# Moving four groups of DMA issues in a one-core hybrid attention/mLSTM layer

## The chip, the cores and the metric

The kernel runs on one core of a Trainium2 chip, as one launch. The metric is the device time of a launch in microseconds (us), lower is better. A time is the median of several runs; one further run is taken with the hardware profiler, and its trace is what the profile shows.

## The reference

One layer of a bidirectional hybrid encoder: 2048 tokens of width 1024. A conditioning vector gives shift, scale and gate; the normalised input goes through one wide projection, whose columns feed two head groups with SiLU gates; one output projection, the residual, and a last RMSNorm follow.

```python
def reference(x, c, w_ada, b_ada, norm_w, w_in, b_in, conv_w, conv_b, rpb, ml_norm_w, w_out, final_norm_w):
    shift, scale, gate = jnp.split(silu(c) @ w_ada + b_ada, 3, axis=-1)
    h = rmsnorm(x, norm_w) * (1 + scale) + shift
    (na_q, na_k, na_v, na_z, ml_q, ml_k, ml_v, ml_o, ml_z, i_f, f_f, i_b, f_b) = split(h @ w_in + b_in)
    # 8 heads of 64: each token attends to 8 x 16 neighbours on a 32 x 64 grid, with a bias table
    na_out = neighbourhood_attention(na_q, na_k, na_v, rpb) * silu(na_z)
    # 4 heads of 128, in both directions; a short centred convolution on q and k first
    mq, mk = split(silu(centred_short_conv(concat(ml_q, ml_k), conv_w, conv_b)))
    hm = (mlstm(mq, mk, ml_v, i_f, f_f) + flipped mlstm(mq, mk, ml_v, i_b, f_b)) * sigmoid(ml_o)
    ml_out = headwise_norm(hm) * ml_norm_w * silu(ml_z)
    y = concat(na_out, ml_out) @ w_out
    return rmsnorm(x + gate * y, final_norm_w)
```

`mlstm` is a chunked recurrence: a state matrix per head is carried from chunk to chunk with a decay, and each chunk adds a masked product of its own queries, keys and values.

## The kernel before

**Number format.** The wide products take three matmuls for one: activations and weights are each split into a high and a low part (`hhi`/`hlo`, `whi`/`wlo`), and high·high, high·low and low·high are added up in PSUM. A weight block is loaded raw by DMA, ScalarE (ACT) copies out the high part, VectorE (DVE) or GpSimd (POOL) subtracts to get the low one.

**Stages, in order of time.** (1) `start`: modulation, norm, transposes and the first two token blocks. (2) The token stage, `tok_blocks`: blocks 2 to 5, each four groups of four token tiles; a token tile is 24 matmuls into one of four `pp` buffers and a DVE addition into a stage tile. Blocks 2 and 3 are mLSTM values and output gates (`vo_group`), blocks 4 and 5 the attention values V (`nav_group`, line 607 the addition, line 611 the store to `d_vna`). The stage tile alternates between two buffers, so the additions of a group wait until the store of the group before the last has landed. After each token tile one step of `self.chain` runs: first `gate_chain`, then `decays`. (3) `conv_blocks`: mLSTM keys and queries with their convolution, and the tables of attention biases (line 679). (4) `phase1b`: the mLSTM passes. Pass 1 builds the states of a head, pass 2 goes through its 16 chunks from c = 15 down to 0 and combines. Beside them `pump` puts out matmuls of a second product, `nq_gen`. (5) `phase2`: attention, 64 units in slots, with the output projection pumped in.

**Decays.** For each of 16 (head, group) pairs `decays` has a 128 x 1024 tile: loaded from `d_mneg` by two DMAs on SyncE's queue, SP (line 833), masked by POOL (841), exponentiated by ACT (845), stored to `d_ck` on ACT's queue (847). Two tiles take turns; the load of pair n + 2 goes into the tile that pair n leaves, and so waits until its store has landed.

**The side product.** `nq_gen` goes through a list of turns, 31 of them; a turn is one weight block of 128 columns and one to four of the groups of 512 tokens, and each of the 64 items (turn, group) is 24 matmuls on line 1001: for k = 0 to 7 the three of `(whi, hhi)`, `(whi, hlo)`, `(wlo, hhi)`, numbered n = 0 to 2. The last seven turns have one group each, but for one of two. The raw weights of the turn after next are held in a single buffer (`rawq`, tag raw0): at k = 2, n = 0 of the first item of a turn `nq_split` (lines 974/975, or 977/978 for the query weights, which it also scales) makes the next turn's halves of `whi_a` and `wlo_a`, and right after it `nq_load` (966) loads the raw weights of the turn after, when the split has read the buffer. The last of these loads, here called the last raw load, is that of turn 30; it is issued in item 61 and split in item 62.

**Pass 2.** Each chunk loads a `ck` tile on SP (1198). `load_z` (1207), also on SP, loads a tile `zt` of z for four chunks into one of two buffers and waits there for an older `zt` to be stored to `d_mix`.

**What sets the order.** DMAs are issued by the queues of SP, ACT and POOL, each in one fixed order, and a DMA that must wait holds up all behind it on its queue. Only `start` and the slots of `phase2` stand under `manual_schedule`; there every engine's order is that of the source. Everywhere else a planner makes each engine's order when the program is built: it follows its own estimate of when an instruction's inputs and buffers are ready, and source order decides between those that are ready together. The manual part of `phase2` begins in the middle of item 59 of the side product: slots 0 to 3 each put out a unit's scores (`stage_s`), the loads for later slots, and then `pump(22)`, 22 matmuls of the side product; slot 4 puts out the rest.

In slots 0 to 2 SP's order after the scores is

```python
load_tab(follows[u], j)          # 1457: bias table of a later unit, two per slot
load_q(n // 2 + 2)               # 1394, 1397: queries, three DMAs, in slot 2
1: [load_w(4), load_w(5)],       # 1460: rows of the output projection, hlo<-d_wo
2: [load_w(6), load_w(7), nc.sync.dma_start(zs[1], self.d_mix[b0])],   # 1460, 1629
```

and then whatever the pumped items issue.

Of the kernel before, what the change touches and what calls it, by code (L numbers as in the profile page):

```python
# [54 lines left out]
def patch_ps(ap):  # L55
    return ap.rearrange("p (a r k) -> p r a k", a=4, k=16)
# [6 lines left out]
class Kernel:  # L63
# [536 lines left out]
    def nav_group(self, blk, slot, g):  # L600
        nc = self.nc
        c0 = (blk - 4) * 256
        st = self.stage_tile(f"stv_{blk}_{g}")
        for o in range(4):
            ps = self.pp.tile([P, GT], F32, tag="pp", name=f"pv_{blk}_{g}_{o}")
            self.tok_tile(ps[:, :256], self.wslot[slot], 4 * g + o)
            nc.vector.tensor_add(st[:, o, :256], ps[:, :256], self.brows[blk % 2])  # L607
            next(self.chain, None)
        self.flush()
        dst = self.d_vna[g * GT : (g + 1) * GT, c0 : c0 + 256].rearrange("(o p) c -> p o c", p=P)  # L610
        self.defer(lambda: nc.sync.dma_start(dst, st[:, :, :256]))

# [203 lines left out]
    def decays(self, pool, beside):  # L816

        nc = self.nc
        mask = pool.tile([P, 2, CH], F32, name="mask")
        nc.gpsimd.memset(mask, 0.0)  # L820
        nc.gpsimd.affine_select(out=mask[:, 0, :], in_=mask[:, 0, :], pattern=[[1, CH]], compare_op=ALU.is_ge, fill=-BIG, base=0, channel_multiplier=-1)
        nc.gpsimd.affine_select(out=mask[:, 1, :], in_=mask[:, 1, :], pattern=[[-1, CH]], compare_op=ALU.is_ge, fill=-BIG, base=0, channel_multiplier=1)
        groups = [(h, gi) for h in range(MH) for gi in range(NG)]
        tiles = {}

        def load(n):
            h, gi = groups[n]
            flat = pool.tile([P, D], F32, tag=("wgate", "gacc")[n % 2], bufs=1, name=f"dec_{h}_{gi}")
            t = flat.rearrange("p (d c t) -> p d c t", d=2, c=4)
            for d in range(2):  # L830
                r = d * 64 + h * NC + 4 * gi
                src = self.d_mneg[:, r : r + 4].rearrange("e r t -> e (r t)").unsqueeze(1).broadcast_to([16, 8, 512])
                nc.sync.dma_start(flat[:, d * 512 : (d + 1) * 512], src)
            tiles[n] = t

        load(0)
        load(1)
        yield
        for n, (h, gi) in enumerate(groups):
            t = tiles.pop(n)  # L840
            nc.gpsimd.tensor_tensor(t, t, mask.unsqueeze(2).broadcast_to([P, 2, 4, CH]), ALU.add)  # L841
            for d in range(2):
                for o in range(4):
                    c = 4 * gi + o
                    nc.scalar.activation(t[:, d, o, :], t[:, d, o, :], AF.Exp, bias=self.cols["g"][:, d, h, c : c + 1])  # L845
                dst = self.d_ck[h, 4 * gi : 4 * gi + 4, :, 641 + d * CH : 641 + (d + 1) * CH].rearrange("c p t -> p c t")
                nc.scalar.dma_start(dst, t[:, d])
            yield
            next(beside, None)
            yield  # L850
            if n + 2 < len(groups):
                load(n + 2)
            yield
        for _ in beside:
            pass

# [123 lines left out]
    def nq_gen(self):  # L980
        nc = self.nc
        whi, wlo = self.wslot[0]
        both, upper, lower = range(NG), (3, 2), (1, 0)
        turns = [(s, both) for s in (0, 1, 2, 3)] + [(s, upper) for s in (4, 5, 6, 7, 8, 9, 10, 11, 12, 14, 13, 15)]
        turns += [(s, lower) for s in (8, 9, 10, 11, 4, 5, 6, 7)]
        turns += [(15, (1,)), (13, (1,)), (14, (1,)), (12, (1, 0)), (14, (0,)), (13, (0,)), (15, (0,))]
        order = [(i, s, g) for i, (s, gs) in enumerate(turns) for g in gs]
        needs = [i for i, (s, gs) in enumerate(turns) if i == 1 or i > 1 and s != turns[i - 2][0]]
        raw = self.nq_load(needs[0], turns[needs[0]][0])
        late, parity = [], False  # L990
        for i, s, g in order:
            off = (i % 2) * P
            kind, ct = ("mz", "nz", "k", "q")[s // 4], s % 4
            patch = kind != "k"
            col = {"mz": 20, "nz": 8, "k": 4, "q": 0}[kind] + ct
            bias = self.bcol[:, col : col + 1]
            ps = self.pp.tile([P, GT], F32, tag="pp", name=f"pq_{s}_{g}")
            for k in range(KT):
                w1, w2 = whi[:, k, off : off + P], wlo[:, k, off : off + P]
                for n, (w, h) in enumerate(((w1, self.hhi), (w1, self.hlo), (w2, self.hhi))):  # L1000
                    nc.tensor.matmul(patch_ps(ps) if patch else ps, w, self.htok(h, g, k, patch), start=(k == 0 and n == 0), stop=(k == KT - 1 and n == 2))  # L1001
                    if k == 2 and n == 0:
                        while late:
                            (nc.gpsimd if self.attention else nc.scalar).dma_start(*late.pop(0))
                    if k == 2 and n == 0:
                        if needs and needs[0] == i + 1:
                            needs.pop(0)
                            self.nq_split(*raw)
                            if needs:
                                raw = self.nq_load(needs[0], turns[needs[0]][0])  # L1010
                    if k < KT - 1 or n < 2:
                        yield
            if kind == "k" and g in lower:

                for j in range(2):
                    rows, other = slice(j * HD, (j + 1) * HD), slice((1 - j) * HD, (2 - j) * HD)
                    cols = slice(j * T + g * GT, j * T + (g + 1) * GT)
                    hv = self.kk[ct][rows, cols]
                    nc.scalar.activation(hv, ps[rows], AF.Identity, bias=bias[rows])
                    nc.vector.scalar_tensor_tensor(self.kk[ct][other, cols], ps[rows], bias[rows], hv.bitcast(F32), ALU.add, ALU.subtract)  # L1020
                yield
                continue
            parity = not parity
            if parity:
                both = self.qst.tile([P, 1032], F32R, tag="st", name=f"qst_{s}_{g}")
            else:
                both = self.raw.tile([P, 1024], F32R, tag="raw1", name=f"qst_{s}_{g}")
            hv, lv = both[:, 0:512], both[:, 512:1024]
            if kind in ("mz", "nz"):
                hv = hv.bitcast(F32)  # L1030
                nc.scalar.activation(hv, ps, AF.Silu, bias=bias)
                dst = self.d_zna[4 * g : 4 * g + 4, :, ct].rearrange("a p q -> p a q") if kind == "nz" else self.d_zml[ct, g]
                nc.scalar.dma_start(dst, hv.rearrange("p (a q) -> p a q", a=4))
                self.zdone.add((kind, ct, g))
            else:
                nc.scalar.activation(hv, ps, AF.Identity, bias=bias)
                nc.vector.scalar_tensor_tensor(lv, ps, bias, hv.bitcast(F32), ALU.add, ALU.subtract)
                for e, part in enumerate((hv, lv)):
                    src = part.bitcast(F32).rearrange("p (a q) -> p a q", a=4)
                    if kind == "q":  # L1040
                        dst = self.d_qna[e, ct // 2, 4 * g : 4 * g + 4, :, ct % 2].rearrange("a p q -> p a q")
                    else:
                        dst = self.d_kna[e, ct * P : (ct + 1) * P, g * GT : (g + 1) * GT].rearrange("p (a q) -> p a q", a=4)
                    late.append((dst, src))
            if (s, g) in ((15, 3), (15, 2)):
                self.freed.append(g)
            yield
        while late:
            nc.gpsimd.dma_start(*late.pop(0))
# [141 lines left out]
    def ml_pass2(self, ml, h):  # L1191
# [11 lines left out]
        def load_z(gi):  # L1203
            while ("mz", h, gi) not in self.zdone:
                self.pump(1)
            t = ml.tile([P, 4, CH], F32, tag="zt", bufs=2, name=f"zt_{h}_{gi}")
            nc.sync.dma_start(t, self.d_zml[h, gi])
            zt[gi] = t
# [87 lines left out]
        last = NC - 1  # L1296
# [6 lines left out]
        for c in range(last, -1, -1):  # L1303
# [5 lines left out]
                scores(c - 1)  # L1309
                weigh(c - 1)  # L1310
            self.pump(PUMP2 / 2)
            if c % 4 == 0:
                load_z(c // 4)
            combine(c)
            if c < last:
                moments(c + 1)
# [469 lines left out]
```

## Time and profile before

| what | us |
|---|---|
| runs | 1330.75, 1332.98, 1333.43 |
| median | 1332.98 |
| the profiled run, as timed | 1336.63 |
| its span, first to last instruction | 1334.6 |
| outside the span | 2.0 |
| DVE busy in it | 781.6 |
| ACT busy in it | 592.9 |
| POOL busy in it | 236.1 |

The profiled run is 3.65 us above the median; differences are worked out inside it and then put on the median. A row of a timeline gives the start, the duration, the engine (a q behind it: its issuing queue), the line, and what is written and read; a bracket holds idle time before the instruction and what ended it. A row of waits gives the waiter, the releaser, the total, the count and the longest. A row of windows gives, for a stretch of time, the busy time of each engine with its instructions in brackets, then TensorE's granted clock, the busy share of the 16 DMA engines (it can pass 1, as packets overlap) and GB/s.

### The profile page before, as it was taken

To read this page: it belongs to the slowest core of one execution; us is meant where nothing else is said; L and a number is where in the kernel's file an instruction comes from. 1 tells how busy PE (TensorE), PEld (TensorE's weight loads), DVE (VectorE), ACT (ScalarE), POOL (GpSimd) and SP (SyncE) were. 2 spreads that over 40 slices of the span, in tenths; PEclk is the share of its full clock that TensorE was granted. 3 is DMA by queue.
4 is the path that set the end of the run, shared out by engine and by line. 5 is a ranking of instruction groups with operands and counts; after the bars stand their busy time and mean duration, and the time that the engine had idled before them with its cause. 6 is when DMAs were issued, how large, how long until landed. Compare 5 with 4: busy or idle time off the path is not lost.

```text
span 1334.6 us, 22971 instructions
## 1 busy us (share of the span) xinstructions
PE 1296.0 (97%) x7934; PEld 1110.7 (83%) x7934; DVE 781.6 (59%) x2466; ACT 592.9 (44%) x1298; POOL 236.1 (18%) x330
## 2 busy tenths in 40 slices
PE   7999999998999999999999999999998999999997
PEld 6899999998888788888888788788776888888885
DVE  7643323111445695157678677777566776777673
ACT  6874446432222332233443433533355555554552
POOL 1001132333011000010211211201442211112110
PEclk9999999999999999999999999999999999999999
DMA  9996488667278875345657779646798887766762
GB/s 370 300 312 152 118 248 226 187 174 201 83 150 226 191 194 176 118 133 159 190 170 220 211 212 261 182 127 178 206 269 239 196 196 186 195 187 174 183 161 78
DMA packets 213128, 258.30 MB, mean 194 GB/s; under 512 B 32026, under 2 KB 164906, under 8 KB 213014
## 3 DMA queue, kind: packets, MB, share of 16 engines
q1 hardware_dynamic: 133238, 172.84, 46.3%
q0 software_dynamic: 25536, 48.86, 14.4%
q10 hardware_dynamic: 54240, 35.15, 9.1%
q8 instruction: 63, 1.03, 0.3%
q14 instruction: 51, 0.42, 0.1%
HBM read 171.25 MB, written 93.71 MB: 199 GB/s over the span
## 4 chain that ended last, share of the span: by engine, by line
PE 68%; DMA 16%; issue 5%; DVE 4%; ACT 3%; POOL 2%; SPq 1%; POOLq 0%; ACTq 0%; DVEq 0%
PE pq L1001 20%; PE y L1564 12%; PE pvo L348 5%; PE pO L1526 4%; PE pT L1511 4%; PE pc L574 3%; PE pc L572 3%; PE pc L573 3%; DMA dec<-d_mneg 3%; DMA d_ck<-dec 2%; DMA wmod<-in_w_mod_dram 2%; DMA d_ck<-acc_k 2%; PE dc L1174 2%; PE pi L1227 2%; PE pvo L572 2%
## 5 line engine op out<-in xcount | busy, mean ns | idle before, releaser
L1001 PE MATMUL pq<-hhi,wlo_a 128*128 128x512 f32 x512 | 210.2, 411 | 1.1 <-DVE wlo_a L978 1.1
L1001 PE MATMUL pq<-hhi,whi_a 128*128 128x512 f32 x512 | 209.7, 410 | 1.1 <-ACT whi_a L977 1.1
L1001 PE MATMUL pq<-hlo,whi_a 128*128 128x512 f32 x512 | 209.6, 409 | 0.0
L1490 ACT ACTIVATE pbuf<-pbuf,mn 128x480 f32<-128x480 f32 (+5 forms) x128 | 76.3, 597 | 105.7 <-DVE mn L1489 105.5
L1001 PEld LDWEIGHTS pq<-hhi,wlo_a 128*128 128x128 f32 x512 | 96.9, 189 | 19.7 <-DVE wlo_a L978 1.9
L1001 PEld LDWEIGHTS pq<-hhi,whi_a 128*128 128x128 f32 x512 | 96.9, 189 | 19.0 <-ACT whi_a L977 1.5
L1001 PEld LDWEIGHTS pq<-hlo,whi_a 128*128 128x128 f32 x512 | 96.9, 189 | 17.5
L1230 ACT ACTIVATE num<-px,gtile 128x129 f32<-128x129 f32 x120 | 38.4, 366 | 107.1 <-PE px L1225 95.8
L1564 PE MATMUL y<-hhi,whi_a 128*128 128x512 f32 x256 | 85.1, 401 | 0.5 <-ACT hhi L1464 0.5
L1564 PE MATMUL y<-hhi,wlo_a 128*128 128x512 f32 x256 | 84.4, 399 | 0.0
L1489 DVE CUSTOM_DVE_ANT_0 pbuf<-pS,tab 128x480 f32<-128x480 f32 (+5 forms) x128 | 64.8, 540 | 30.6 <-PE pS L1484 22.2
L1249 POOL TENSOR_TENSOR hm<-hm,ck 128x128 f32<-128x128 f32 x64 | 30.2, 471 | 249.7 <-DVE hm L1248 195.7
L845 ACT ACTIVATE dec<-dec,gtile 128x128 f32<-128x128 f32 x128 | 41.6, 391 | 70.4 <-POOL dec L841 67.8
L1144 POOL DMA_DIRECT2D kv<-d_ck x64 | 34.6, 541 | 194.7 <-PE dc L1174 92.3
L1526 PE MATMUL pO<-turned,v 128*64 128x128 f32 (+3 forms) x832 | 60.7, 280 | 2.8 <-DVE sums L1499 1.5
L607 DVE TENSOR_TENSOR stv<-pv,brow 128x256 f32<-128x256 f32 x32 | 12.6, 422 | 84.0 <-DMA d_vna<-stv 42.0
L1526 PEld LDWEIGHTS pO<-turned,v 128*64 128x64 f32 (+3 forms) x832 | 44.7, 136 | 19.5 <-issue 13.6
L1511 PE MATMUL pT<-ident,pbuf 128*128 128x128 f32 (+2 forms) x416 | 59.1, 280 | 0.5 <-DVE pbuf L1501 0.5
L1513 ACT ACTIVATE turned<-pT 96x384 f32<-96x384 f32 (+3 forms) x128 | 57.8, 501 | 1.1 <-PE pT L1511 0.7
L1564 PEld LDWEIGHTS y<-hhi,whi_a 128*128 128x128 f32 x256 | 47.4, 188 | 9.9 <-ACT hhi L1464 0.8
L1564 PEld LDWEIGHTS y<-hhi,wlo_a 128*128 128x128 f32 x256 | 47.5, 188 | 9.1
L1511 PEld LDWEIGHTS pT<-ident,pbuf 128*128 128x128 f32 (+2 forms) x416 | 43.7, 136 | 11.6 <-issue 9.5
(331 smaller groups left out, 3517.8 us busy)
## 6 DMA issues: line engine op xcount, KB each, us to landing
ck<-d_ck SPq DMA_DIRECT2D x64, 384.5 KB
rawq<-in_w_side_dram SPq DMA_DIRECT2D x30, 512.0 KB
raw<-in_w_main_dram SPq DMA_DIRECT2D x20, 512.0 KB
kv<-d_ck POOLq DMA_DIRECT2D x64, 128.5 KB, 2.9
x<-in_x_dram SPq DMA_DIRECT2D x16, 512.0 KB
dec<-d_mneg SPq DMA_DIRECT2D x32, 256.0 KB
d_ck<-dec ACTq DMA_DIRECT2D x32, 256.0 KB
xr<-in_x_dram POOLq DMA_DIRECT2D x16, 512.0 KB, 8.3
```

The costliest lines, as they stand in the source:

```text
L348: nc.tensor.matmul(ps[:, :width], m, w[:, k, :width], start=(h == 0 and k == 0 and high and w is hi), stop=last)
L572: nc.tensor.matmul(ps, lhi(k), rhi(k), start=(k == 0), stop=False)
L573: nc.tensor.matmul(ps, lhi(k), rlo(k), start=False, stop=False)
L574: nc.tensor.matmul(ps, llo(k), rhi(k), start=False, stop=(k == KT - 1))
L845: nc.scalar.activation(t[:, d, o, :], t[:, d, o, :], AF.Exp, bias=self.cols["g"][:, d, h, c : c + 1])
L1001: nc.tensor.matmul(patch_ps(ps) if patch else ps, w, self.htok(h, g, k, patch), start=(k == 0 and n == 0), stop=(k == KT - 1 and n == 2))
L1489: nc.vector.tensor_tensor_reduce(pt[:, :nk], ps, tabs[place[u]][j][:, :nk], 1.0, 3e38, ALU.add, ALU.min, mn)
L1490: nc.scalar.activation(pt[:, :nk], pt[:, :nk], AF.Exp, bias=mn, scale=-1.0, accum_out=sums[:, j : j + 1])
L1511: nc.tensor.transpose(ps[:cs, i, :], pts[j][:, i * cs : (i + 1) * cs], self.ident)
L1513: nc.scalar.activation(t[:cs, :nch, :], ps[:cs, :nch, :], AF.Copy)
L1526: nc.tensor.matmul(po[j * HD : (j + 1) * HD, :], v[:n, h * HD : (h + 1) * HD], pt[j][:n, i, :], start=(i == 0), stop=(i == nch - 1))
L1564: nc.tensor.matmul(y, m[:, k, :], w[k][:, cs], start=(k == 4 and n == 0), stop=(k == 3 and n == 2))
```

## The change

Four places are edited; no instruction is added or taken away. In `nav_group` the store of the group before is issued after the second token tile of a group, not after the fourth. In `decays` the load of pair n + 2 is issued one step of the chain later. In `nq_gen` a raw load no longer follows the split at k = 2 but comes at k = 7, or at k = 4 where the block is needed in the turn after next and the next turn has one group. In pass 2 `load_z` is called one chunk later, at c = 11, 7, 3 and, as before, at 0.

```diff
@@ nav_group
             nc.vector.tensor_add(st[:, o, :256], ps[:, :256], self.brows[blk % 2])
+            if o == 1:
+                self.flush()
             next(self.chain, None)
-        self.flush()
@@ decays
             yield
             next(beside, None)
             yield
+            yield
             if n + 2 < len(groups):
                 load(n + 2)
-            yield
@@ nq_gen
                             needs.pop(0)
                             self.nq_split(*raw)
-                            if needs:
-                                raw = self.nq_load(needs[0], turns[needs[0]][0])
+                            raw = None
+                    if raw is None and needs and n == 0 and k == (4 if needs[0] == i + 2 and len(turns[i + 1][1]) == 1 else 7):
+                        raw = self.nq_load(needs[0], turns[needs[0]][0])
@@ ml_pass2
-            if c % 4 == 0:
-                load_z(c // 4)
+            if c % 4 == 3 and c != last:
+                load_z(c // 4 + 1)
+            elif c == 0:
+                load_z(0)
             combine(c)
```

## The prediction

> **What bounds the kernel now.** First the page: engines' busy time. Then who TensorE (PE) waited for, since only idle PE can be won or lost.
>
> ```profile
> span 1334.6 us, 22971 instructions
> PE 1296.0 (97%) x7934; PEld 1110.7 (83%) x7934; DVE 781.6 (59%) x2466; ACT 592.9 (44%) x1298; POOL 236.1 (18%) x330
> ```
>
> ```profile
> PE pv L572 <- DVE stv L607: 3.4, 1, 3.4
> PE a L1212 <- DMA ck<-d_ck: 2.8, 3, 1.6
> PE pvo L572 <- DVE stvo L627: 2.6, 2, 1.3
> ...
> PE pq L1001 <- ACT whi_a L977: 1.1, 1, 1.1
> PE pq L1001 <- DVE wlo_a L978: 1.1, 2, 0.5
> ```
>
> PE is busy 97% of the span and in order, so it is the bound; 38.6 us are left idle in all. The change adds and removes no instruction, so busy time stays. What it can move is waits. In the second fence the first and third rows are the token stage (a full set of PSUM buffers), the second is pass 2, and the last two are the side product waiting for its split weights. These five come to 11.0 us.
>
> A stall also costs clock. The stretches behind the 3.4 us stall:
>
> ```profile
> 315.50:318.70 3.20, 3.06 (x14) 3.06 (x15) 1.08 (x4) 2.67 (x8) 0.10 (x1) 0.50 1.08 321
> 318.70:321.90 3.20, 3.20 (x29) 3.20 (x29) 0.42 (x1) 0.00 (x0) 0.00 (x0) 0.99 0.96 141
> ```
>
> The third number from the right (0.50, 0.99) is the granted clock. At half clock 14 matmuls start in 3.20 us, at full clock 29: 15 matmuls at 3.20 / 29 = 0.11 us, so 1.6 us lost.
>
> **The edits that the planner decides.** The V store, the decay loads, z and all raw loads but the last stand outside the manual slots. Does their place in the source set their place on SP's queue?
>
> ```profile
> 220.89 0.67 SPq L679 DMA_DIRECT2D d_t<-d_e  x1
> ```
>
> ```profile
> 309.86 0.66 SPq L679 DMA_DIRECT2D d_t<-d_e  x1
> 310.62 0.41 SPq L611 DMA_DIRECT2D d_vna<-stv  x1
> ```
>
> These are SP's timelines. Line 679 belongs to the convolution stage, behind every V group in the source, yet it is issued at 220.89 and again at 309.86, right ahead of a V store (L611). Had the planner held that store ready, it would have gone first, as it stands earlier in the source. So the store goes when the planner thinks its additions are done, and an earlier flush gives it a rank it doesn't need. The same holds for loads that get a later rank: nothing of a rank between old and new stands ready behind them, as far as SP's order shows. I take 0 us for these edits. Bounds: the V store and the decay loads can win the 3.4 and 2.6 us and one half-clock spell (1.6), the raw and z loads the 2.8 us of `ck`: 10.4 us won at most. Against it, one more stall like the worst, 3.4 + 1.6 = 5.0 us lost. The cover that makes 0 is the four PSUM buffers, and the two-group turns between raw loads; where it goes, PE waits as in the rows above.
>
> **The last raw load, which source order decides.** In the slots the source rules. SP's timeline there:
>
> ```profile
> 969.31 0.92 SPq L1460 DMA_DIRECT2D hlo<-d_wo  x2
> 974.18 0.33 SPq L966 DMA_DIRECT2D rawq<-in_w_side_dram  x1
> 974.62 1.26 SPq L1457 DMA_DIRECT2D tab<-d_t  x2
> 975.97 0.63 SPq L1394 DMA_DIRECT2D qhigh<-d_qna  x1
> 976.71 1.23 SPq L1397 DMA_DIRECT2D qlow<-d_qna  x2
> 977.98 1.87 SPq L1460 DMA_DIRECT2D hlo<-d_wo  x2
> 983.38 0.32 SPq L1629 DMA_DIRECT2D gtile<-d_mix  x1
> ```
>
> ```profile
> 974.94 0.48 PE L1001 MATMUL pq<-hhi,wlo_a 128*128 128x512 f32 x1
> ```
>
> The last raw load goes out at 974.18, after the split at k = 2, n = 0 of item 61, which is late in slot 1's `pump(22)`. Only one more matmul (n = 1) fits that pump. Slot 2's pump opens, in the second fence, with `wlo`, that is n = 2 of k = 2. So k = 4, n = 0 is its fifth matmul, and the new place of the load lies behind everything that slot 2 issues on SP: two tables, three query loads, two `hlo` loads, the mix load. It is moved past eight DMAs. How soon does it land?
>
> ```profile
> SPq L1629 <- DMA rawq<-in_w_side_dram: 3.5, 1, 3.5
> ```
>
> ```profile
> hlo<-d_wo SPq DMA_DIRECT2D x4, 512.0 KB
> ...
> tab<-d_t SPq DMA_DIRECT2D x6, 180.0 KB
> ...
> rawq<-in_w_side_dram SPq DMA_DIRECT2D x1, 512.0 KB
> ```
>
> ```profile
> 983.40:986.00 2.60, 2.60 (x13) 2.12 (x12) 1.98 (x2) 2.48 (x3) 0.00 (x0) 1.00 1.06 265
> 986.00:988.00 2.00, 1.47 (x7) 0.89 (x6) 2.00 (x3) 0.69 (x1) 0.19 (x1) 1.00 1.03 400
> 988.00:990.00 2.00, 2.00 (x21) 1.56 (x20) 1.36 (x6) 0.76 (x3) 1.89 (x3) 1.00 1.06 368
> 990.00:992.00 2.00, 2.00 (x13) 1.71 (x11) 1.41 (x5) 1.90 (x5) 0.11 (x1) 1.00 0.76 229
> ```
>
> Today the mix load waits for its landing, so it landed just ahead of 983.38: 9.2 us after issue, behind two `hlo` loads. In the windows the DMA engines are full (second number from the right over 1) up to 990, and have room after. The bytes are the same after the change; the last raw load only goes from the front of this full stretch to its end. I take its landing as the end of the stretch, **990.0**. Bounds: it is issued at about 980 at the earliest, behind SP's 977.98 + 1.87. Alone at 265 GB/s its 512 KB would take 2 us, so 982 from below, which costs nothing; from above, the tables, the `hlo` loads and itself (2 x 180, 2 x 512 and 512 KB), 1.9 MB, at half of 265 GB/s, the other half POOL's, take 14 us from 980: 994. The load waits for no engine there, as its buffer was read by 974.2, so what stands behind it on SP, tables of a later slot, comes no later than now; today it stands behind the mix load's wait.
>
> What it delays:
>
> ```profile
> 982.93 2.00 ACT L1464 ACTIVATE hhi<-hlo 128x1024 fp32r<-128x1024 f32 x2
> 984.83 1.06 ACT L977 ACTIVATE whi_a<-rawq 128x1024 fp32r<-128x1024 f32 x1
> ```
>
> ```profile
> 986.29 1.22 DVE L978 SCALAR_TENSOR_TENSOR wlo_a<-rawq,whi_a 128x1024 fp32r<-128x1024 f32 x1
> ```
>
> ```profile
> 986.40 0.40 PE L1001 MATMUL pq<-hhi,whi_a 128*128 128x512 f32 x1
> ...
> 987.57 0.51 PE L1001 MATMUL pq<-hhi,wlo_a 128*128 128x512 f32 x1 [0.53 <-DVE wlo_a L978]
> ```
>
> ACT splits at 984.83, 1.45 us after the landing, because L1464 is ahead of it; that is all the slack. PE reaches item 63 at 986.40 and already waits 0.53 us for the low part. With a landing at 990.0: ACT 990.05 to 991.1, DVE 991.1 to 992.35, PE's third matmul at 992.4 where it was 987.57: **+4.8 us**. PE is in order, so slot 4's scores wait too. On ACT the eviction of item 62 and the next exponentials queue behind L977, on DVE the rest of slot 4; both wait for PE's scores anyway. POOL's later loads follow item 63's eviction and shift with it.
>
> PE idles from about 986.4 to 991.1 in one piece. Shorter gaps have dropped the clock:
>
> ```profile
> 955.00 0.50 PE L1001 MATMUL pq<-hhi,whi_a 128*128 128x512 f32 x1 [1.07 <-ACT whi_a L977]
> ```
>
> ```profile
> 957.00:960.40 3.40, 3.40 (x10) 2.69 (x10) 2.21 (x4) 1.44 (x2) 0.23 (x1) 0.51 0.87 193
> ```
>
> A 1.07 us wait (and one of 0.5 after it) was followed by 3.40 us at 0.51. I add one half-clock spell, 1.6 us. The Trainium skill ("TensorE: Matmul & The Clock Gate", Part 1, the HAM clock gate) has it otherwise: half rate only after a whole idle window of about 3.4 us, on a window that runs freely; the row at 957 does not agree, being reached without such an idle window. By that rule a gap of 4.7 us might pass without a drop, and the time would be rival 1's.
>
> **Sum.** 0 + 4.8 + 1.6 = +6.4 us: profiled time 1336.63 to 1343.0 (span 1341.0), and on the median of the runs 1332.98 + 6.4 = **1339.4**.
>
> **Rivals.**
> 1. The clock holds. PE's stall of 4.8 us alone: 1337.8. For it: no drop is seen in every short wait of the table. Against: the two spells above.
> 2. The load is hidden: SP reaches it at 980, and its packets pass quickly. It decides at a landing of 985 (983.38 plus the 1.45 us slack): earlier than that nothing moves, 1333.0. Against: full DMA engines until 990. That the planner's edits do nothing is part of this rival and of the forecast.
> 3. Faster: the planner does follow the source, the V store lands before the buffers are full and `ck` no longer queues behind z. With the last load's cost, 6.4 - 10.4 = -4.0: 1329.0; without it 1322.6. It wins when more than 6.4 of the 10.4 us come. Against: the L679 rows.
> 4. Worse: the landing at 994, which is 4 us more, or another 5.0 us stall in the token stage: 1332.98 + 6.4 + 4 to 5 = 1343.4 to 1344.4.
>
> **How the numbers follow.** Forecast 0.52; rival 1 0.15; rival 2 0.18; rival 3 0.08; rival 4 0.07. A measurement can tell about 0.2%, 2.7 us, from no change: 1330.3 to 1335.6. Forecast, 1 and 4 are slower: 0.74. Rival 2 is the same: 0.17 of it; a little of it and rival 3 are faster: 0.09. The forecast's own range, landing 988.5 to 992, is 1336.3 to 1341.4; the range reaches to 1332 for most of rival 2, and to 1343.5 for a late landing.
>
> **What would show it.** On SP the rawq load after L1629, at about 980; its landing, by ACT's start on L977, near 990; a PE wait of near 5 us on ACT L977 at item 63, and a half-clock spell after it. In the token stage the order of L611 and L679 as now, and the 3.4 us wait still there. The prediction is wrong if L977 starts before 986.4, or if the token stage's waits go.

## The result, and the profile after

| | before | after |
|---|---|---|
| median of the runs, us | 1333.23 (7 runs, 1330.75 to 1335.68) | 1344.81 (7 runs, 1337.25 to 1345.41) |
| profiled execution, us | 1336.63 | 1345.17 |
| its span, us | 1334.6 | 1343.3 |

The ratio after to before is 1.0057, with a 95% interval of 1.0034 to 1.0081: 7.6 us slower on 1333.23, 4.5 to 10.8. It is not the quotient of the two medians, which lie 11.6 us apart: the runs of after fall into two groups, three from 1337.25 to 1339.49 and four from 1344.81 to 1345.41, and the median is the lowest of the upper four. So the direction is sure, the size only to several microseconds. The forecast was +6.4 us, slower. The median of after lies 1.3 us over the upper end of the range; why is told below.

**What the change did to the program.** Put side by side instruction by instruction, the two traces have the same order on PE, DVE, ACT, GpSimd and SP, but for one transfer: the last raw load, rawq_30, stands eight places later on SP. The V stores, the decay loads, the z loads and the other raw loads are where they were. So whatever differs between the two traces ahead of that load is not the change.

The page of after, its span and its engines:

```profile
span 1343.3 us, 22970 instructions
...
PE 1301.7 (97%) x7934; PEld 1115.3 (83%) x7934; DVE 781.6 (58%) x2466; ACT 592.0 (44%) x1298; POOL 234.9 (17%) x330
```

The same matmuls are busy for 5.7 us longer (1296.0 before): matmuls that ran at half clock. The other 3 us of the span are waits.

SP's timeline in after (start, duration, instruction), where before had the raw load ahead of all of these:

```profile
977.61 0.85 SPq L1461 DMA_DIRECT2D tab<-d_t  x2
978.55 0.64 SPq L1398 DMA_DIRECT2D qhigh<-d_qna  x1
979.28 1.45 SPq L1401 DMA_DIRECT2D qlow<-d_qna  x2
980.78 1.05 SPq L1464 DMA_DIRECT2D hlo<-d_wo  x2
981.88 0.65 SPq L1633 DMA_DIRECT2D gtile<-d_mix  x1
984.30 0.33 SPq L967 DMA_DIRECT2D rawq<-in_w_side_dram  x1
```

Eight transfers first, as worked out. Then SP waits once more, which was not worked out: the group of waits of SP for that line shows the landing of a table.

```profile
SPq L967 <- DMA tab<-d_t: 1.7, 1, 1.7
```

ACT's timeline in after, the split of the weights that the load brings:

```profile
992.38 1.06 ACT L978 ACTIVATE whi_a<-rawq 128x1024 fp32r<-128x1024 f32 x1 [4.39 <-DMA rawq<-in_w_side_dram]
```

ACT has nothing to do for 4.39 us but wait: the load landed at 992.4, 8.1 us behind its issue. PE's timeline of the same place, before and then after; the last row of each is the first scores matmul of slot 5:

```profile
985.01 0.40 PE L1001 MATMUL pq<-hhi,whi_a 128*128 128x512 f32 x1
...
985.71 0.39 PE L1001 MATMUL pq<-hhi,whi_a 128*128 128x512 f32 x1
...
1000.04 0.32 PE L1483 MATMUL pS<-hhi,qhigh 128*128 128x360 f32 x1
```

```profile
988.07 0.40 PE L1002 MATMUL pq<-hhi,whi_a 128*128 128x512 f32 x1
...
988.76 0.39 PE L1002 MATMUL pq<-hhi,whi_a 128*128 128x512 f32 x1
...
993.49 0.80 PE L1002 MATMUL pq<-hhi,whi_a 128*128 128x512 f32 x1 [3.87 <-ACT whi_a L978]
...
994.75 0.80 PE L1002 MATMUL pq<-hhi,wlo_a 128*128 128x512 f32 x1
...
1009.34 0.32 PE L1487 MATMUL pS<-hhi,qhigh 128*128 128x360 f32 x1
```

Before, PE takes 1000.04 - 985.01 = 15.03 us from the first of these matmuls to the last; after, 1009.34 - 988.07 = 21.27 us. **The change costs 6.24 us in this stretch.** PE's idle time in it grows from 0.53 us to 3.9, nearly all of it the wait in brackets: 3.4 us more. The other 2.9 us are matmuls at half clock, as the windows of after show (third number from the right: granted clock):

```profile
988.00:992.00 4.00, 1.62 (x8) 0.97 (x6) 1.43 (x2) 0.00 (x0) 0.00 (x0) 1.00 0.97 374
992.00:996.00 4.00, 2.48 (x5) 1.57 (x6) 1.89 (x2) 1.63 (x2) 0.90 (x2) 0.58 0.07 27
996.00:1000.00 4.00, 4.00 (x24) 3.19 (x24) 2.32 (x9) 1.46 (x5) 1.28 (x2) 0.57 0.74 197
```

The last row has 0.57 where PE works all of the time. Behind the stretch nothing more is lost: the next 300.1 us of before, up to 1300, take 299.6 in after. Below, this stretch is the measure of what the moved load costs: it is the same matmuls in every kernel (number 5690 to 5776 in PE's order, with 16 more in the run that fills the wait), and in nine of the ten experiments that left the load in time it took 15.01 to 15.04 us (15.32 in the tenth, the last one).

In the token stage the wait that the edits aim at is still there, and so is the order of SP's timeline that the prediction quoted:

```profile
PE pv L572 <- DVE stv L607: 3.1, 1, 3.1
```

```profile
307.40 0.67 SPq L680 DMA_DIRECT2D d_t<-d_e  x1
308.17 0.40 SPq L612 DMA_DIRECT2D d_vna<-stv  x1
```

### The profile page after: what moved, and what is told of

It is laid out like the page before. It is cut to its first block, busy times and chain, and to the rows that moved or that the text cites. A ratio compares the mean times of both kernels' runs of the same rounds, so it can differ in the third digit from the quotient of the medians.

```text
span 1343.3 us, 22970 instructions
## 1 busy us (share of the span) xinstructions
PE 1301.7 (97%) x7934; PEld 1115.3 (83%) x7934; DVE 781.6 (58%) x2466; ACT 592.0 (44%) x1298; POOL 234.9 (17%) x330
## 4 chain that ended last, share of the span: by engine, by line
PE 70%; DMA 17%; DVE 3%; issue 3%; ACT 3%; POOL 2%; SPq 1%; ACTq 0%; POOLq 0%; DVEq 0%
PE pq L1002 21%; PE y L1568 12%; PE pvo L348 5%; PE pO L1530 4%; PE pT L1515 4%; PE pc L573 3%; PE pc L574 3%; PE pc L572 3%; DMA d_ck<-dec 2%; DMA wmod<-in_w_mod_dram 2%; DMA dec<-d_mneg 2%; PE pi L1229 2%; DMA d_ck<-acc_k 2%; PE px L1227 2%; DMA rawq<-in_w_side_dram 2%
```

## The experiments

Two questions: is the last raw load the whole effect, and through what; and what would the other edits be worth if they did move something. Each time below is the median of its runs, each ratio, with its 95% interval, is to the runs of the kernel before on the same chip. In the first four runs the kernel before itself had a median of 1339.45 over 34 runs (1331.18 to 1346.43), so single times of a few microseconds apart say little; the ratios and the stretch carry the argument. The level differs by chip too: the median of before was 1334.70 where the fifth to eighth run were made, and 1339.18 and 1340.36 for the last two pairs. So the absolute times in the expectations below, set on the 1333 of the first runs, are no measure; the ratios are.

### The last raw load alone

```diff
                         if needs and needs[0] == i + 1:
...
-                            if needs:
-                                raw = self.nq_load(needs[0], turns[needs[0]][0])
+                            raw = None if needs == [30] else self.nq_load(needs[0], turns[needs[0]][0]) if needs else None
+                    if raw is None and needs == [30] and (i, k, n) == (28, 4, 0):
+                        raw = self.nq_load(30, turns[30][0])
```

> The kernel before with one edit: the last raw load (rawq_30) goes from k = 2 to k = 4. V store, decay loads, z loads and the other raw loads stay as they were before. Theory A (the last raw load is the whole effect of the change): +5 to +12 us on the kernel before, as the whole change had (1337 to 1346); PE waits 3 to 5 us on ACT's split at item 63, and the half clock follows that wait. Theory B (the other edits cost time too): less than half of the loss, so at most 1338, and the rest must show in the next run. Spells of half clock ahead of 970 us lie before the edit: if they come and go between this profile and that of the whole change, they are chance.

Measured: 1344.22 us, ratio 1.0041 (1.0020 to 1.0061), so +5.5 us (2.7 to 8.2). On SP, ACT and PE:

```profile
979.88 0.33 SPq L966 DMA_DIRECT2D rawq<-in_w_side_dram  x1
```

```profile
988.45 1.06 ACT L977 ACTIVATE whi_a<-rawq 128x1024 fp32r<-128x1024 f32 x1 [5.31 <-DMA rawq<-in_w_side_dram]
```

```profile
989.56 0.80 PE L1001 MATMUL pq<-hhi,whi_a 128*128 128x512 f32 x1 [4.79 <-ACT whi_a L977]
```

The load lands 8.6 us behind its issue, PE waits 4.79 us, 6.83 us at half clock begin at 987.40, and the stretch takes 21.61 us. Theory A holds: one moved transfer makes the loss. By the order of its trace this program is that of the whole change, so the two profiles are two draws of one program. The spells of half clock ahead of 980 are not the same in them: at 313.37, 839.02 and 968.73 in the first, at 314.98 alone in the second. Those are chance, and are part of the first profile's 8.7 us of span over before.

### The whole change but for that load

```diff
                             self.nq_split(*raw)
-                            raw = None
+                            raw = self.nq_load(30, turns[30][0]) if needs == [30] else None
```

> The whole change, but the last raw load stays at k = 2 as before. Theory A: the time of the kernel before within 0.2% (1330 to 1336), no wait over 1 us on ACT's split at item 63, the 3.4 us wait in front of 312 us still there. Theory B: slower than before by over 3 us.

Measured: 1339.54 us, ratio 1.0006 (0.9984 to 1.0028), stretch 15.04 us. PE's waits:

```profile
PE pv L572 <- DVE stv L607: 3.8, 2, 2.9
...
PE pvo L572 <- DVE stvo L628: 2.1, 3, 1.5
```

All four edits that the planner decides, together, change nothing: the waits that they aim at stand there as before.

### The same late place, but another queue

The edit is shown against the first run.

```diff
-                        raw = self.nq_load(30, turns[30][0])
+                        raw = self.nq_load(30, turns[30][0], nc.scalar)
...
-        nc.sync.dma_start(raw, self.w_side[s])
+        (queue or nc.sync).dma_start(raw, self.w_side[s])
```

> As the first run (last raw load at k = 4), but this one load is issued by ACT and not by SP, so that it stands neither behind the eight transfers of slot 2 nor behind SP's wait for a landing (issued at 984.30 after 1.7 us of waiting in the changed kernel). Theory A (the place on SP's queue makes the loss): ACT issues it at about 979, it lands ahead of 988, PE waits under 1 us at item 63, and the time is that of before within 0.3% (1329 to 1337). Rival C (the load is late because the DMA engines are full, whoever issues it): landing after 990 as before this edit, PE waits 3 us or more, and the loss stays at +5 us or more.

Measured: 1337.96 us, ratio 0.9998 (0.9976 to 1.0019), stretch 15.03 us. ACT's queue and then ACT, in one timeline:

```profile
977.46 0.38 ACTq L966 DMA_DIRECT2D rawq<-in_w_side_dram  x1
...
986.92 1.05 ACT L977 ACTIVATE whi_a<-rawq 128x1024 fp32r<-128x1024 f32 x1
```

At the same place in the source, the load leaves 11 us ahead of the matmul that needs it (988.50), where in the first run it left 4.7 ahead, and ACT does not wait. The loss is gone, so it is not the step in the source but what stood in front of the load on SP. That ACT's queue also carries a load faster is not shown: the load had 9.5 us until ACT read it, and took 8.6 in the first run. Rival C, the full DMA engines, falls, as they are as full here (second number from the right):

```profile
984.00:988.00 4.00, 4.00 (x21) 3.35 (x20) 2.75 (x6) 3.97 (x7) 0.00 (x0) 1.00 1.07 278
```

### The wait filled with matmuls

```diff
+                    if (i, k, n) == (30, 0, 0):
+                        for _ in range(16):
+                            nc.tensor.matmul(ps, self.hhi[g][:, 0, 0:P], self.hhi[g][:, 0, :], start=True, stop=True)
                     nc.tensor.matmul(patch_ps(ps) if patch else ps, w, ...
```

> As the first run, with 16 extra matmuls (128x512, on data that is in SBUF, into item 63's PSUM tile, overwritten at once) ahead of item 63's first matmul, so that PE works through the wait for the late load instead of idling (16 x 0.232 us = 3.7 us at full clock). They add work to the kernel, none is left out. Theory D (the idle stretch itself drops the clock, and the two half-clock windows behind it, 6.83 us, cost about 3.3 us): the spell behind item 63 is gone, and the time is 2.5 to 4 us under the first run's. Rival E (the spell comes whatever PE does there, or its cost is small): within 1.5 us of the first run, or slower where the extra matmuls reach past the landing.

Measured: 1343.91 us, ratio 1.0031 (1.0007 to 1.0054). Against the first run's 1.0041 that is 0.3 us apart in the medians and 1.3 us in the ratios, inside the spread of both, so the times decide nothing. The stretch does. PE's timeline and the windows:

```profile
984.86 3.79 PE L1003 MATMUL pq<-hhi 128*128 128x512 f32 x16
989.86 0.51 PE L1004 MATMUL pq<-hhi,whi_a 128*128 128x512 f32 x1 [1.22 <-ACT whi_a L977]
...
991.12 0.50 PE L1004 MATMUL pq<-hhi,wlo_a 128*128 128x512 f32 x1 [0.52 <-DVE wlo_a L978]
```

```profile
988.00:992.00 4.00, 2.26 (x9) 1.27 (x8) 1.89 (x2) 1.63 (x2) 0.64 (x1) 1.00 0.16 59
992.00:996.00 4.00, 4.00 (x31) 3.24 (x30) 2.60 (x10) 3.12 (x8) 1.55 (x3) 1.00 0.57 149
```

PE is held at item 63 for as long as in the first run (3.79 + 1.22 = 5.01 us, 4.79 there), but works through most of it, and the clock stays at 1.00. The stretch takes 20.14 us, 1.47 less than the 21.61 of the first run. So the idle time itself drops the clock (the first half of theory D), but the drop costs 1.5 us here, not the 3.3 that I had put on two windows; in its price rival E was right. Part of the first window lies in the wait, where a slow clock costs nothing. What is left of the loss, 20.14 - 15.03 = 5.1 us, is the late load alone.

### Half as far back

```diff
+                            if needs == [30]:
+                                raw = []
+                                self.issue_late = lambda: raw.extend(self.nq_load(30, turns[30][0]))
-                            if needs:
+                            elif needs:
...
-            2: [lambda: load_w(6), lambda: load_w(7), ...
+            2: [lambda: self.issue_late(), lambda: load_w(6), lambda: load_w(7), ...
```

> The kernel before, with the last raw load half as far back: in slot 2 behind its two tables and three query loads, but ahead of its two hlo loads and the mix load. Measured by the stretch of PE from the anchor of item 61 to that of slot 5 (15.03 us before, 21.27 with the whole change, 21.61 in the first run). Theory G (the load lands 8 to 9 us behind its issue, wherever it stands: 9.1 before, 8.1 in the change, 8.5 in the first run): issue near 978, landing near 986.7, PE waits 1 to 2 us in all at item 63 where it waits 0.5 before, stretch 15.5 to 17 us (up to 18.5 with a drop of the clock), total within +0.5 to +3.5 us of before. Rival F (it lands with the end of the stretch of full DMA engines, wherever it stands in it): landing near 990, stretch 20 to 22 us, total +5 us or more.

Measured: 1333.65 us, ratio 0.9999 (0.9976 to 1.0021), stretch 15.03 us. SP, then ACT:

```profile
975.79 0.54 SPq L966 DMA_DIRECT2D rawq<-in_w_side_dram  x1
```

```profile
983.01 1.06 ACT L977 ACTIVATE whi_a<-rawq 128x1024 fp32r<-128x1024 f32 x1 [0.20 <-DMA rawq<-in_w_side_dram]
```

The load lands 7.2 us behind its issue and just in time: ACT waits 0.20 us, PE no longer than before. Rival F is out. Theory G priced the landing 1.5 us too late, and the 0.5 us or more that it expected the stretch to lose did not come: with only five small transfers ahead of it and the 1 MB of the two hlo loads behind, the load is quicker than the 8 to 9 us of the other places. Five places back cost nothing, eight cost 6 us: what lies between is the two hlo loads, the mix load and the wait for a table's landing; which of them weighs most was not taken apart and stays open.

### V stores on another queue

```diff
-        self.defer(lambda: nc.sync.dma_start(dst, st[:, :, :256]))
+        self.defer(lambda: nc.scalar.dma_start(dst, st[:, :, :256]))
```

> What the change means to do in the token stage, done in another way: the kernel before, with the stores of the navigation V stages (L611) issued by ACT and not by SP, so that they cannot stand behind decay loads that wait for a landing. Theory H (SP's order makes the 3.4 us wait of PE ahead of 312): that wait is under 1 us, the stretch of PE from 300 to 330 on the clock of before takes 27 us or less (30.06 before, 28.15 to 31.16 in the other profiles, 26.76 at best), and the total is 2 to 5 us under before. Rival I (the store itself or DVE is late): the wait stays over 2 us, total within 0.2%; or ACT is held up by the store's wait and the loss shows behind 330.

Measured: 1340.68 us, ratio 1.0033 (1.0014 to 1.0051): slower. The stretch from 300 to 330 takes 35.31 us, where before took 30.06. ACT's timeline:

```profile
309.81 1.57 ACT L845 ACTIVATE dec<-dec,gtile 128x128 f32<-128x128 f32 x5 [11.41 <-POOL dec L841]
...
312.96 1.09 ACTq L611 DMA_DIRECT2D d_vna<-stv  x1
```

Theory H fails in this form, but is not refuted: ACT waits 11.41 us for a decay tile, and the store stands behind that as it stood behind the decay load on SP. PE's waits on stv grow to 7.3 us in two pieces. Rival I had expected the store to hold up ACT; here ACT's work holds up the store.

For the next run the mLSTM stages' stores (L634) go to ACT too, by the same edit there.

> As the run before, and the stores of the mLSTM V stages (L634) on ACT too, where ACT's sigmoid (L631) has just made the data. Theory H: the waits of PE on stvo at 207 and 214 (1.3 us each before) go as well; the stretch from 200 to 220 takes 18.5 us or less (20.01 before), and the total is 3 to 7 us under before. Rival I: the waits stay, or ACT's evictions are held up and the total is not under before.

Measured: 1335.08 us, ratio 1.0001 (0.9982 to 1.0020). PE's waits:

```profile
PE pv L572 <- DVE stv L607: 3.2, 1, 3.2
...
PE pvo L572 <- DVE stvo L627: 0.2, 1, 0.2
```

The waits on stvo go (stretch 200 to 220: 16.85 us, 20.01 before), the one on stv stays. The total does not show the 3 us, and its interval (-2.4 to +2.7 us) has hardly room for them. The seven profiles whose order in this stage is that of before spread from 18.41 to 21.25 us in this stretch, so the gain may be as little as 1.6 us.

### Decay loads on GpSimd

```diff
-                nc.sync.dma_start(flat[:, d * 512 : (d + 1) * 512], src)
+                nc.gpsimd.dma_start(flat[:, d * 512 : (d + 1) * 512], src)
```

> The other way to take the decay loads from in front of the V stores: the loads of the decay tiles (L833) are issued by GpSimd, whose mask addition is what waits for them anyway; the stores stay on SP. Theory H: SP no longer stands in a decay load (6.67 us at 302 before), the 3.4 us wait ahead of 312 is under 1 us, total 2 to 5 us under before. Rival J (GpSimd waits for the landing in its place, and its memset of the stages or its split of weights comes late): a new wait of PE on a POOL line, total not under before.

Measured: 1359.44 us, ratio 1.0192 (1.0157 to 1.0226), far slower. GpSimd's timeline, then SP's:

```profile
252.71 1.05 POOL L833 DMA_DIRECT2D dec<-d_mneg  x2 [3.90 <-ACT dec L845]
253.75 4.66 POOL L209 TENSOR_TENSOR wlo_b<-raw,whi_b 128x1024 fp32r<-128x1024 f32 x2
```

```profile
256.15 0.35 SPq L200 DMA_DIRECT2D raw<-in_w_main_dram  x1
...
264.43 0.38 SPq L611 DMA_DIRECT2D d_vna<-stv  x1
```

GpSimd waits 3.90 us to issue a decay load; its split of the weights (L209) comes late, SP's raw loads wait for that split's buffers, and the V store is behind them. Rival J, by a detour: PE's wait is still named stv, 25.7 us in four pieces.

### The edits where source order rules

In the next two runs the token stage is taken out of the planner's hands; the second also has the change's edits.

```diff
-        self.tok_blocks(self.pool(toks, "chain", bufs=1, side="right"))
+        with tc.manual_schedule():
+            self.tok_blocks(self.pool(toks, "chain", bufs=1, side="right"))
```

> The kernel before, with the token stage (blocks 2 to 5) taken out of the planner's hands: there the source order is the order on each engine and queue. The control for the next run. On SP the decay loads then stand in front of the V stores as the source of before has them. Expected: PE's wait ahead of 312 stays at 2 us or more; stretches of PE 200 to 220, 220 to 300 and 300 to 330 on the clock of before (20.01, 79.99 and 30.06 us) of 18 to 22, 79 to 83 and 28 to 36 us; total between -3 and +10 us of before, as the planner's other choices are lost too.

> The run before with the change's edits in it (V store flushed in mid-group, decay loads a step later, last raw load at its old place): now the edits do move the stores ahead of the decay loads on SP. Theory K (the edits are right and the planner alone made them void): the waits of PE on stv and stvo (three waits, 6.0 us in the kernel before) fall to under 2 us in all, the three stretches take at least 3 us less than in the run before, and the total is 2 to 6 us under it. Rival L (the stall comes from the landing of stores and decay tiles on full DMA engines, whatever SP's order): the waits stay over 3 us, total within 2 us of the run before.

Measured: 1366.28 us, ratio 1.0210 (1.0183 to 1.0238), without the edits; 1358.31 us, ratio 1.0150 (1.0116 to 1.0184), with them. PE's waits without, then with:

```profile
PE pv L573 <- DVE stv L608: 10.4, 2, 7.5
PE pv L573 <- DVE stvo L628: 7.4, 1, 7.4
...
PE gp L562 <- DVE wide L564: 3.2, 1, 3.2
```

```profile
PE pv L573 <- DVE stvo L629: 6.5, 1, 6.5
PE pv L573 <- DVE stv L608: 5.3, 3, 3.7
```

The stretch from 200 to 330 takes 152.7 us without and 141.4 us with the edits. So the edits shorten PE's waits, by 11 us in the stretch and 8 us in the total, once their order reaches the queue (theory K in its sign; the waits stay far above the 2 us that I had expected). Which of the edits does it was not taken apart. But the planner's order is worth 28 us, more than the edits; I had expected 10 at most.

The control also missed in another way. PE's wait ahead of 312, which I had expected to stay, is gone without the edits: the stretch from 300 to 330 takes 24.99 us without them and 25.60 with them, where before took 30.06. The waits in the rows above are others, all ahead of that stretch, and one of them is new, that on the small product of the gate (`gp`).

### Source order for one block

```diff
+                elif blk == 4:
+                    self.nav_group(blk, blk % 2, g)
                 else:
-                    self.nav_group(blk, blk % 2, g)
+                    with self.tc.manual_schedule():
+                        self.nav_group(blk, blk % 2, g)
```

> The change with its last raw load at the old place, and the V groups of block 5 alone in source order; the rest of the token stage stays with the planner. There the flush in mid-group and the later decay loads put each V store ahead of the decay load that SP waits in. Theory K (the edits pay where their order is kept): the wait of PE ahead of 312 (3.4 us before) is under 1 us, the stretch from 300 to 330 on the clock of before takes 24.5 to 26.5 us (30.06 before, 28.15 to 31.16 in the other profiles of that order), the other stretches as before, total 2 to 5 us under before. Rival M (the planner gives the gain back elsewhere, as the source order of the whole stage did: 19 us in the stretch 220 to 300): that stretch over 83 us or that from 420 to 470 over 53, total not under before.

Measured: 1340.57 us, ratio 1.0002 (0.9986 to 1.0018). The wait ahead of 312 is gone, the stretch from 300 to 330 takes 25.00 us (30.06 before), and the stretch from 220 to 300 takes 85.17 (79.99 before): 5.1 us won and 5.2 us lost, rival M. That the edits won the 5.1 us is not shown: source order alone took away the same wait in the run without them. PE's waits name the new one, on the gate's product (L561), which that run had too:

```profile
PE gp L561 <- DVE wide L563: 2.7, 1, 2.7
...
PE pv L572 <- DVE stv L607: 0.5, 1, 0.5
```

The last run adds the mLSTM stages' stores on ACT.

> As the run before, with the stores of the mLSTM V stages (L634) on ACT as well, which took away the waits on stvo (stretch 200 to 220 of 16.85 us for 20.01). Theory K: the two gains add up, both stretches short (16.9 and 24.5 to 26.5 us), total 4 to 8 us under before (0.3 to 0.6%), the fastest of the study. Rival M: one of the waits comes back, as the planner lays SP's order anew, total within 0.2% of before.

Measured: 1337.29 us, ratio 0.9986 (0.9974 to 0.9998), 1.9 us under before (0.3 to 3.5), the only ratio of the study whose interval ends below 1. One such interval among twelve is weak evidence, and the gain is less than the 0.2% that I can tell with confidence. The stretch from 300 to 330 is short again (25.03 us), the one from 200 to 220 is not (19.01), since the planner laid the rest anew:

```profile
PE pvo L572 <- DVE stvo L628: 4.2, 2, 2.3
PE kt L959 <- ACT acc_k L949: 3.5, 2, 3.1
```

Not tried: the z loads and the earlier raw loads in source order, as their stage is the planner's too.

## Why the prediction was right, point by point

**The edits that the planner decides: 0 us.** Right, and shown twice: by the two programs, whose orders differ in one transfer, and by the run without that transfer (ratio 1.0006). The L679 rows told it in advance. What they could not tell is that the edits are worth 11 us in their stretch under source order. That this lies near the bound of 10.4 us is chance: the bound was added up from the waits of before, and the waits under source order are others (17.8 us in the first two rows).

**The last raw load: +4.8 us.** The place on SP was right, eight transfers back and behind the mix load. The issue was later than the 980 taken: SP also waited 1.7 us for a table's landing, and the load left 5.2 us ahead of the end of item 62 (984.30 against 988.76 + 0.69) where the prediction had 6.4. The landing came 2.9 us behind that point, 3.8 in the second draw; 990.0 on the clock of before meant 3.6. From item 62's last high-part matmul to item 63's third matmul before took 987.57 - 985.71 = 1.86 us and after 994.75 - 988.76 = 5.99: +4.13, and +5.05 in the second draw. The 4.8 lies between the two, with some luck: the load left later than I took, and took 8.1 and 8.6 us from issue to use where I had put 10, and the two errors partly cancel. The term left out was SP's own wait. The reason that I gave for the landing, the end of the stretch of full DMA engines, holds for the last place in the queue only: from the middle of it the load landed 7.2 us behind its issue, with that stretch still running.

**One half-clock spell: +1.6 us.** The spell came in both draws. It lasted two windows of 3.41 us and not one, but began inside the wait; behind the third matmul it cost 6.24 - 4.13 = 2.1 us and 21.61 - 15.03 - 5.05 = 1.5 us. That two windows, one of them partly hidden, cost about what I had put on one is luck. Filling the wait with matmuls took the spell away and 1.47 us with it. The rule cited from the Trainium skill ("TensorE: Matmul & The Clock Gate", Part 1), half rate after at least one idle window, would have let the clock hold if that window must be idle as a whole. Here the window ahead of the spell was 0.88 idle in the one draw and 0.77 in the other, so the rule read in that way does not agree with these traces.

**Sum.** Forecast +6.4; the stretch gave +6.24 and +6.58, the ratios +7.6 (4.5 to 10.8) and +5.5 (2.7 to 8.2). The rivals "the clock holds" and "the load is hidden" are out; "the planner follows the source" too.

**The upper end of the range.** The median of after was 1344.81, over 1343.5, while the ratio on 1332.98 gives 1340.6, inside the range. The step that failed is the conversion to the runs: I put the sum on the median of three runs, 1332.98, as if runs of this kernel agreed to a microsecond. On one chip, 34 later runs of the kernel before had a median of 1339.45 and went from 1331.18 to 1346.43; on another, 29 runs had a median of 1334.70. The range should have held that spread as well.

## What to carry to other kernels

Where a planner sets the order of a queue, an edit of the source order is no change until the compiled order shows it: compare the two orders first, and price only what moved. A load that is moved by a few matmuls in the source moves on its queue past everything that another slot issues in between, and is in time or late by what stands there: count the transfers, and those that wait themselves. A gain belongs to an edit only if the same order without the edit still has the wait. Where a total scatters by half a percent, take the time between the same two matmuls in both traces; here nine kernels agreed to 0.03 us in it, where the totals could not tell 3 us.

## What the hardware did that was not expected

The drops of the clock keep to a grid. In each profile all spells of half clock begin a whole number of windows of 3.413 us apart, and, but for the one in which a program ends, last one to four of them (in after, 839.02 - 313.37 = 525.65 us is 154 windows). I laid that grid over 13 profiles (all but the one without a spell in the middle of the kernel) and took PE's idle time in each window between 60 us and some 10 us before the end, where every one of these programs finishes at half clock. Of the windows at full clock, 4724 were at most 45% idle, and none was followed by half clock; 27 were more than 55% idle, and all were; of the 22 between, 10 were. Of the windows at half clock, the 37 that were at most 15% idle were followed by full clock, the 15 that were over 20% idle by half clock again. So a wait of under 2 us can be enough, where it falls into one window, and one of 3 us may pass, where it is cut in two. PE's waits in the run with the load on ACT's queue show both:

```profile
PE pv L572 <- DVE stv L607: 2.9, 1, 2.9
...
PE pvo L572 <- DVE stvo L627: 2.3, 2, 1.8
```

Behind the 1.8 us (at 213.6) half clock began at 215.78; behind the 2.9 us (at 313.4) none did. The Trainium skill ("TensorE: Matmul & The Clock Gate", Part 1) has a free-running window of this length, and there the traces agree; that it must be idle as a whole they don't show. All this is read from the traces; one experiment only, the filled wait, tested it (no window over 36% idle there, and no drop).

It would explain a part of the scatter of the runs: the grid does not start with the program, the seven profiles with the order of before hold five to nine waits of PE of 0.9 us or more each, and which of them cost a window changes from run to run. The granted clock noted for each run bears this out: over the 34 runs of before, a mean clock lower by 0.001 goes with 1.2 us more (correlation 0.64), and one half-clock window of 3.41 us in a span of 1335 lowers the mean by 0.0013 and costs about 1.5 us. It is not all of the scatter: at a noted clock of 0.994 those runs went from 1336.06 to 1344.20. What else moves them, and why the median differs by chip, is open. The two draws of the changed program had seven and three such windows in the middle of the kernel, at about 1.5 us each.
